# Last FFN of a four-layer trunk: column pairs of its first product by Strassen's seven products, and the second product's weights loaded by use

## The chip, the cores and the metric

One Trainium2 chip, one of its cores. The kernel is launched once. Its time is the device time of that launch in microseconds (us), and lower is better. Engines are named as in the profile: PE is TensorE (matmuls; PEld its weight loads), DVE is VectorE, ACT is ScalarE, POOL is GpSimd, SP is SyncE, whose queue issues most DMAs.

## What is computed

Two layers of an encoder trunk over 512 tokens of 1024 features: a mixer (a short convolution in the first layer, a chunked state-space mixer in the second) and a feed-forward network (FFN) after each, all float32. The change is in the last FFN:

```python
D_MODEL, SEQ, D_FF = 1024, 512, 2816
def swiglu_ffn(h, w_in, w_out):
    gate, up = jnp.split(h @ w_in, 2, axis=-1)
    return (jax.nn.silu(gate) * up) @ w_out
# for each layer, after its mixer:
h = rmsnorm(x, norm_g[i, 2]) * (1.0 + scale) + shift
x = x + gate * rmsnorm(swiglu_ffn(h, f_w_in[i], f_w_out[i]), norm_g[i, 3])
```

`h @ w_in` (512 x 1024 by 1024 x 5632) is called the first product here, the product with `w_out` (512 x 2816 by 2816 x 1024) the second. In the kernel `w1` is `w_in` and `w2` is `w_out` of the last layer.

## The kernel before

**Matmuls in three parts.** A float32 operand is split into a rounded high part (a copy to the type fp32r, on ACT) and the rest (a subtraction on DVE). A product is then three matmuls: high by high, high by low, low by high (`mm3`, L275 to L278). So every weight tile costs an ACT copy and a DVE subtraction of the same size before TensorE can use it.

**First product.** 44 chunks of 128 columns (22 for the gate, 22 for the up half). A chunk (`in_chunk`, L289) is 8 blocks of 128 features times three matmuls of all 512 tokens, accumulated in one PSUM bank. Six chunks (`lead_ps`) are begun in the boundary ahead of the stage with 256 tokens at a time and ended by `rest` (L1678). Two more (`more`) have their weights ready. The other 36 come in 18 pairs: `load_pair` (L1580) loads 256 columns, 1 MB, into a staging tile `wst` (a pool of two), and the splits run two chunks ahead of TensorE. `gate` (L1583) puts SiLU of a gate chunk into a temporary, `up` (L1591) multiplies the up chunk with it into `raw`, and `s13` (L1587) forms sums of `raw` for the second product.

**Second product.** It runs by Strassen's scheme already: `w2` in four blocks b11 to b22, the activations in a11 to a22, 7 products of 11 pairs each, 77 steps of 6 matmuls of 512 columns (`products`, L1639). `w_prep` and `a_prep` split what a pair of steps (a number n from 0 to 38) needs, some steps ahead. The sums of weight blocks are made by DMAs of the POOL queue that add while they write, `add_` (L1656), with the names `t1`, `t2_`, `t3`, `t4`; `behind(n)` (L1743) places them and the output arithmetic by n. `w2` lies in units of one or two pairs (`units`, nine of them): units 0 to 2 in `w2t` tiles, loaded at chunks 8, 14 and 20 of the first product, 3 and 4 in the staging pool near its end, and 5 to 8 in the space of `h` once the first product is over (L1705 to L1710). `t3` needs b12 + b22 in b11's place: ACT's queue loads the one (`t3_load`) and POOL adds the other from memory.

**Order.** In this stage all five engines run in the written order (`manual_schedule`, L1653): on each engine and on each queue an instruction that waits holds up all that stand behind it. A tile that takes the place of an older one waits until the older one's last reader is done.

## Time and profile before

| | |
|---|---|
| three timed runs | 1356.21, 1356.53, 1357.03 us (median 1356.53) |
| profiled execution: span from the first to the last instruction | 1355.3 us, 17419 instructions |
| mean granted TensorE clock | 0.997 |
| HBM read | 192.75 MB |
| plain loads of 1 MB of `w1` | 16 after 1030 us, 5.2 us from issue to landing |
| accumulating DMAs (POOL queue) | 38, 11.54 MB |

The execution was taken by the hardware profiler; only its span is given, and the timed runs lie 1.2 us above it in the median. L12 is line 12 of the kernel. A row of a group gives line, engine, operation, tiles written and read, shape and count, then the busy time and the mean duration in ns, then the idle time just before such instructions and what ended it. A row of the timeline gives start, duration, and in brackets the idle time before it and what ended it; "issue" is a wait for nothing that the profile shows as data. Six columns of a stretch are its length and the busy us of the engines with instruction counts, then the granted clock, the DMA engines' busy share and GB/s.

### The profile page before, as it was taken

To read this page: it belongs to the slowest core of one execution; us is meant where nothing else is said; L and a number is where in the kernel's file an instruction comes from. 1 tells how busy PE (TensorE), PEld (TensorE's weight loads), DVE (VectorE), ACT (ScalarE), POOL (GpSimd) and SP (SyncE) were. 2 spreads that over 40 slices of the span, in tenths; PEclk is the share of its full clock that TensorE was granted. 3 is DMA by queue.
4 is the path that set the end of the run, shared out by engine and by line. 5 is a ranking of instruction groups with operands and counts; after the bars stand their busy time and mean duration, and the time that the engine had idled before them with its cause. 6 is when DMAs were issued, how large, how long until landed. Compare 5 with 4: busy or idle time off the path is not lost.

```text
span 1355.3 us, 17419 instructions
## 1 busy us (share of the span) xinstructions
PE 1339.1 (99%) x6909; PEld 1126.9 (83%) x6909; DVE 898.7 (66%) x1437; ACT 570.1 (42%) x893; POOL 47.0 (3%) x61
## 2 busy tenths in 40 slices
PE   8999999999999999999999999999999999999996
PEld 6788889888888888898888888888899888888885
DVE  5588866777777322658988998897673233336877
ACT  5333355232222211655554455564472212224664
POOL 0000000000000000000000000000000000001231
PEclk9999999999999999999999999999999999999998
DMA  9757760777786323415434334323311455326685
GB/s 311 233 180 231 247 202 4 242 237 245 227 257 201 110 94 94 128 33 162 137 122 128 107 96 132 117 78 121 129 62 63 156 171 172 98 96 196 159 148 120
DMA packets 160565, 204.77 MB, mean 151 GB/s; under 512 B 6868, under 2 KB 112228, under 8 KB 159460
## 3 DMA queue, kind: packets, MB, share of 16 engines
q1 hardware_dynamic: 148512, 176.34, 41.2%
q0 software_dynamic: 6240, 11.54, 5.1%
q10 hardware_dynamic: 5732, 15.79, 3.6%
q8 instruction: 54, 0.88, 0.3%
q14 instruction: 27, 0.22, 0.1%
HBM read 192.75 MB, written 2.24 MB: 144 GB/s over the span
## 4 chain that ended last, share of the span: by engine, by line
PE 93%; issue 2%; SPq 2%; DMA 1%; DVE 1%; ACT 1%; POOL 0%; DVEq 0%; POOLq 0%; ACTq 0%
PE ip L276 19%; PE ip L278 18%; PE ip L277 18%; PE y L378 6%; PE y L379 6%; PE y L380 6%; PE cA L1650 3%; PE li L276 3%; PE li L278 3%; PE li L277 3%; PE li L756 1%; PE yd L1283 1%; PE cD L1650 1%; SPq L611 1%; PE yo L1277 1%
## 5 line engine op out<-in xcount | busy, mean ns | idle before, releaser
L276 PE MATMUL ip<-h,whl 128*128 128x512 f32 x1096 | 431.1, 393 | 0.2 <-DVE cv L863 0.2
L278 PE MATMUL ip<-h,whl 128*128 128x512 f32 x1096 | 427.2, 390 | 0.0
L277 PE MATMUL ip<-h,whl 128*128 128x512 f32 x1096 | 426.8, 389 | 0.0
L222 DVE TENSOR_TENSOR whl<-wst,whl 128x1024 fp32r<-128x1024 f32 x132 | 160.7, 1221 | 133.4 <-ACT whl L221 133.2
L276 PEld LDWEIGHTS ip<-h,whl 128*128 128x128 f32 x1096 | 205.9, 188 | 43.9 <-issue 1.8
L278 PEld LDWEIGHTS ip<-h,whl 128*128 128x128 f32 x1096 | 205.8, 188 | 43.2
L277 PEld LDWEIGHTS ip<-h,whl 128*128 128x128 f32 x1096 | 206.0, 188 | 41.8
L221 ACT CAST whl<-wst 128x1024 fp32r<-128x1024 f32 x132 | 136.6, 1042 | 32.5 <-PE ip L278 23.7
L124 DVE SCALAR_TENSOR_TENSOR ada_acc<-ada_st,csil,ada_acc 128x512 f32<-128x512 f32 x140 | 105.0, 750 | 3.5
L204 DVE TENSOR_TENSOR whlo<-wsto,whlo 128x1024 fp32r<-128x1024 f32 x41 | 49.9, 1224 | 78.5 <-ACT whlo L203 78.4
L276 PE MATMUL li<-h,whl 128*128 128x256 f32 x288 | 83.3, 289 | 0.0
L278 PE MATMUL li<-h,whl 128*128 128x256 f32 x288 | 81.7, 284 | 0.0
L277 PE MATMUL li<-h,whl 128*128 128x256 f32 x288 | 81.6, 283 | 0.0
L203 ACT CAST whlo<-wsto 128x1024 fp32r<-128x1024 f32 x41 | 42.6, 1049 | 76.5 <-PE y L380 71.3
L378 PE MATMUL y<-whlo,ff 128*128 128x512 f32 x176 | 68.7, 390 | 0.0
L380 PE MATMUL y<-whlo,ff 128*128 128x512 f32 x176 | 68.5, 389 | 0.0
L379 PE MATMUL y<-whlo,ff 128*128 128x512 f32 x176 | 68.5, 389 | 0.0
L1142 DVE SCALAR_TENSOR_TENSOR cu<-ip,cols,cu 128x511 f32<-128x511 f32 (+2 forms) x84 | 62.8, 748 | 3.9 <-ACT cu L1139 1.4
L1585 ACT ACTIVATE g<-ip 128x512 f32<-128x512 f32 x18 | 10.8, 598 | 122.1 <-PE ip L278 122.1
L1650 PE MATMUL cA<-whlo,ao 128*128 128x512 f32 x264 | 61.1, 390 | 0.8 <-ACT whlo L1615 0.8
L1650 PEld LDWEIGHTS cA<-whlo,ao 128*128 128x128 f32 x264 | 49.5, 188 | 11.4 <-ACT whlo L1615 1.2
L276 PEld LDWEIGHTS li<-h,whl 128*128 128x128 f32 x288 | 55.3, 192 | 0.0
(281 smaller groups left out, 1928.2 us busy)
## 6 DMA issues: line engine op xcount, KB each, us to landing
ada_st<-in_ada_w_dram SPq DMA_DIRECT2D x96, 512.0 KB, 5.0
wst<-in_f_w_in_dram SPq DMA_DIRECT2D x44, 1024.0 KB, 5.9
wst<-in_m_w_in_dram SPq DMA_DIRECT2D x14, 1024.0 KB, 5.3
wsto<-in_f_w_out_dram SPq DMA_DIRECT2D x10, 1024.0 KB, 5.0
wst<-in_m_w_in_dram SPq DMA_DIRECT2D x20, 512.0 KB, 5.1
wst<-in_a_w_in_dram SPq DMA_DIRECT2D x9, 1024.0 KB, 6.0
csb<-cs_d ACTq DMA_DIRECT2D x8, 1024.0 KB, 5.5
wsto<-in_m_w_out_dram SPq DMA_DIRECT2D x7, 1024.0 KB, 6.5
```

Source lines behind the costliest of these rows:

```text
L124: dve.scalar_tensor_tensor(acc, w, csil[:, k:k + 1], acc, MUL, ADD)
L204: dve.tensor_tensor(dst[:, 1, :nk, :], src, dst[:, 0, :nk, :].bitcast(F32), SUB)
L221: later.append((lambda sw=sw, w=w: act.copy(w[:, 0, :nk, :], sw), lambda sw=sw, w=w: dve.tensor_tensor(w[:, 1, :nk, :], sw, w[:, 0, :nk, : ...
L222: lambda sw=sw, w=w: dve.tensor_tensor(w[:, 1, :nk, :], sw, w[:, 0, :nk, :].bitcast(F32), SUB)))
L276: pe.matmul(dst, w_at(w, 0, kk), a[:, 0, sl], start=start, stop=False)
L277: pe.matmul(dst, w_at(w, 0, kk), a[:, 1, sl], start=False, stop=False)
L278: pe.matmul(dst, w_at(w, 1, kk), a[:, 0, sl], start=False, stop=stop)
L378: pe.matmul(pst, a[:, 0, tk], wt[:, 0, kk, :], start=k == 0, stop=False)
L379: pe.matmul(pst, a[:, 0, tk], wt[:, 1, kk, :], start=False, stop=False)
L380: pe.matmul(pst, a[:, 1, tk], wt[:, 0, kk, :], start=False, stop=k == K - 1)
L1142: dve.scalar_tensor_tensor(u[:, sft:], pst[:, :T - sft], w[3 - sft], u[:, sft:], MUL, ADD)
L1650: pe.matmul(bank[r][sub], a[:, al, q, tk], w[:, hl, q, :], start=first and k == 0, stop=last and k == 2, skip_group_check=True)
```

## The change

The 36 paired chunks become 16 *units* and four plain chunks. A unit is a pair of neighbouring column chunks, gate (even u) or up (odd u). Its four quadrants (feature halves by column chunks) and the four quadrants of `h` (feature halves by token halves, `HALVES`) go through Strassen's seven products P1 to P7, each 4 blocks x 3 matmuls of 256 columns (`product`, `FACTORS`).

- The sums of quadrants of `h` are made once, ahead of the loop: `value` joins high and low part of `h` again, and `t_one` to `t_four` form the four sums and split them into `tq`, which takes the space of `w2t0` and `w2t1`. `va` is a staging tile (`wst`).
- The sums of weight quadrants are made per unit: `fetch(u)` loads five pieces by SP (1.25 MB, rows of 512 bytes) and adds four pieces of 128 KB by `add_` on POOL; `sum_y` and `sum_s` add two more on DVE. `split_x`, `split_y`, `split_z`, `split_s` are the high and low parts of four weight tiles.
- The products of a unit are spread over two turns of the loop (P1, P5, P2, P6, P3 in its own, P7 and P4 in the next). `keep`, `c11`, `c12`, `c22`, `c21` put the four result quadrants together out of three PSUM banks, and end with SiLU or with the product into `raw`.
- All of `w2` is loaded after the units, block by block (`w2_load(i, "b11", ...)`) in the order of use.
- `t3` is a subtraction on POOL (b22 - b11, with b22 already holding the sum) instead of a load and an adding DMA, and stands behind `t4`.

```diff
-        ws, splits, gates = list(more), [(), ()], {}
-        w2t = [fb.tile([P, 2, 2, D], F32, tag=f"w2t{i}", name=f"w2t{i}") for i in range(2)]
-        w2t += [fb.tile([P, 1, 2, D], F32, tag="w2t2", name="w2t2")]
+        gates = {}
+        tq = [fb.tile([P, 2, 2, 4, 256], F32R, tag=f"w2t{i}", name=f"tq{i}") for i in range(2)]
+        sums_w = fb.tile([P, 2, 2, 4, P], F32, tag="w2t2", name="sg")
         raw = fb.tile([P, NF, T], F32, tag="raw", name="raw")
...
+        def w2_load(i, *names):
             u = units[i]
-            t = w2t[i] if i < 3 else wst_p.tile([P, 1, 2, D], F32, tag="wst", name="w2s")
-            for q in range(len(u)):
-                dma(t[:, q, :, :], w2_rows(u[q])[:, 0])
-            rows_of[i] = (t[:, :, 0, :], t[:, :, 1, :])
+            for name in names:
+                r, c = int(name[1]) - 1, int(name[2]) - 1
+                dma(b_(i, name), w2_rows(u[0], len(u))[:, :, r, c * T:(c + 1) * T])
...
+        UN = 16
+        LO, HI = HALVES
+        FACTORS = {"P1": ("X", 0, "A"), "P2": ("X", 4, "B"), "P3": ("S", 0, "C"), "P4": ("Z", 4, "A"),
+                   "P5": ("Y", 0, "C"), "P6": ("Y", 4, "A"), "P7": ("Z", 0, "A")}
+        staged, wts, banks, outs = {}, {}, {}, {}
+        def w1_cols(u, f, kh=None):
+            c0 = u % 2 * DFF + (4 + u // 2 * 2 + f) * P
+            rows = slice(0, D) if kh is None else slice(kh * T, (kh + 1) * T)
+            return w1[rows, c0:c0 + P].rearrange("(k p) f -> p k f", p=P)
+        def add_(dst, src):
+            pool.dma_start(dst, src, accum_op=ADD)
+        def fetch(u):
+            st, sg = wst_p.tile([P, 16, P], F32, tag="wst", name="wsu"), sums_w[:, u % 2]
+            staged[u] = st, sg
+            dma(st[:, 0:8, :], w1_cols(u, 0))
+            if u < UN:
+                dma(sg[:, 0], w1_cols(u, 1, 0))
+            if u:
+                dma(st[:, 8:12, :], w1_cols(u - 1, 0, 0))
+            for b in (0, 2):
+                if u < UN:
+                    add_(sg[:, 0, b:b + 2, :], w1_cols(u, 1, 1)[:, b:b + 2, :])
+                if u:
+                    add_(st[:, 8 + b:10 + b, :], w1_cols(u - 1, 1, 0)[:, b:b + 2, :])
+            if u:
+                dma(st[:, 12:16, :], w1_cols(u - 1, 1, 1))
...
+        def split_x(u):
+            wts["X", u] = whole()
+            split(wts["X", u], staged[u][0][:, 0:8, :])
+        def split_y(u):
+            wts["Y", u] = whole()
+            split(wts["Y", u], staged[u][1].rearrange("p s k f -> p (s k) f"))
+        def split_z(u):
+            wts["Z", u] = whole()
+            split(wts["Z", u], staged[u + 1][0][:, 8:16, :])
+        def split_s(u):
+            wts["S", u] = fo.tile([P, 2, 4, P], F32R, tag="ao", name="wss")
+            split(wts["S", u], staged[u][0][:, 4:8, :])
+        def sum_y(u):
+            st, sg = staged[u]
+            dve.tensor_add(sg[:, 1], sg[:, 0], st[:, 0:4, :])
+        def sum_s(u):
+            st, sg = staged[u]
+            dve.tensor_add(st[:, 4:8, :], sg[:, 1], st[:, 4:8, :])
...
+        def product(u, q):
+            kind, k0, r = FACTORS[q]
+            if q in ("P1", "P5", "P2"):
+                banks[r, u] = (aux_ps if r == "B" else mm_ps)(f"s{r}")
+            dst, w = banks[r, u][:, LO], wts[kind, u]
+            for k in range(4):
+                for i, (wl, al) in enumerate(((0, 0), (0, 1), (1, 0))):
+                    pe.matmul(dst, w[:, wl, k0 + k, :], moving(q, k, al), skip_group_check=True,
+                              start=q in ("P1", "P5", "P2") and k == 0 and i == 0, stop=k == 3 and i == 2)
...
+        def c11(u):
+            dve.tensor_add(out_of(u, 0)[:, LO], banks["B", u][:, LO], out_of(u, 0)[:, LO])
+        def c12(u):
+            o, f = out_of(u, 0), 4 + u // 2 * 2
+            dve.tensor_add(o[:, HI], banks["C", u][:, LO], o[:, HI])
+            if u % 2:
+                dve.tensor_mul(o, o, gates[f])
+            else:
+                gates[f] = o
+                act.activation(o, o, AF.Silu)
...
-            def t3_load(i):
-                for q, p in enumerate(units[i]):
-                    dma_s(b_(i, "b11", q), w2_rows(p)[:, 0, 0, T:])
             def t3(i):
-                for q, p in enumerate(units[i]):
-                    add_(b_(i, "b11", q), w2_rows(p)[:, 0, 1, T:])
+                pool.tensor_tensor(b_(i, "b11"), b_(i, "b22"), b_(i, "b11"), SUB)
...
+            va = wst_p.tile([P, 4, T], F32, tag="wst", name="va")
+            vb = [fo.tile([P, 2, T], F32, tag="ao", name="vb") for _ in range(2)]
+            fetch(0)
+            def value(j):
+                dst = va[:, j, :] if j < 4 else vb[j // 2 - 2][:, j % 2, :]
+                dve.tensor_add(dst, h[j][:, 0, :].bitcast(F32), h[j][:, 1, :].bitcast(F32))
...
+            def t_one():
+                dve.tensor_tensor(va[:, :, LO], va[:, :, LO], va[:, :, HI], SUB)
+                t_low(tq_of(0, slice(0, 4)), va[:, :, LO])
+            def t_two(b):
+                k = slice(2 * b, 2 * b + 2)
+                dve.tensor_tensor(va[:, k, HI], vb[b][:, :, HI], va[:, k, HI], SUB)
+                dve.tensor_add(vb[b][:, :, HI], vb[b][:, :, HI], va[:, k, LO])
+                t_low(tq_of(1, k), vb[b][:, :, HI], -1.0)
+            def t_three():
+                t_low(tq_of(2, slice(0, 4)), va[:, :, HI])
+            def t_four(b):
+                k = slice(2 * b, 2 * b + 2)
+                dve.tensor_tensor(vb[b][:, :, LO], vb[b][:, :, HI], vb[b][:, :, LO], SUB)
+                t_low(tq_of(3, k), vb[b][:, :, LO])
...
             for i, f in ((0, 0), (2, 0), (1, 1), (3, 1), (4, 2), (5, 3)):
                 rest(i)
-                (up if i in (2, 3) else gate)(f, lead_ps[i])
-            tiles = []
-            K = 2 * NF - 6
-            for k in range(K):
-                if k % 2 == 0 and k < K - 4:
-                    load_pair(k // 2 + 1)
-                if k in (8, 14, 20):
-                    w2_load((8, 14, 20).index(k))
-                if k in (K - 4, K - 2):
-                    w2_load(3 + (k - K + 4) // 2)
-                if k in (K - 12, K - 10, K - 8):
-                    t1((k - K + 12) // 2)
-                tiles.append(in_chunk(ws[k], h))
-                q, j = divmod(k - 3, 4)
-                if j < 2 and k > 2:
-                    gate(4 + 2 * q + j, tiles[k - 1])
-                elif k:
-                    up(2 + 2 * q + j, tiles[k - 1])
-                if k < K - 2:
-                    for op in splits[k + 2]:
+                if i in (2, 3):
+                    up(f, lead_ps[i])
+                else:
+                    gate(f, lead_ps[i])
+                if i == 1:
+                    for j in range(4):
+                        value(j)
+                elif i == 3:
+                    t_one()
+                elif i == 4:
+                    for j in range(4, 8):
+                        value(j)
+            acc = in_chunk(more[0], h)
+            split_x(0)
+            for b in range(2):
+                t_two(b)
+            sum_y(0)
+            split_y(0)
+            t_three()
+            fetch(1)
+            acc2 = in_chunk(more[1], h)
+            sum_s(0)
+            up(2, acc)
+            split_s(0)
+            for u in range(UN):
+                v = u - 1
+                last = u == UN - 1
+                if u + 2 <= UN:
+                    fetch(u + 2)
+                elif last:
+                    tail = []
+                    n12 = load_w([(w1, 21 * P, P), (w1, DFF + 20 * P, P)], later=tail)
+                product(u, "P1")
+                if u:
+                    c12(v)
+                else:
+                    up(3, acc2)
+                    for b in range(2):
+                        t_four(b)
+                split_x(u + 1)
+                if u:
+                    product(v, "P7")
+                keep(u, "A", 0, LO)
+                if not last:
+                    sum_y(u + 1)
+                product(u, "P5")
+                if u:
+                    c22(v)
+                product(u, "P2")
+                keep(u, "C", 1, HI)
+                if not last:
+                    sum_s(u + 1)
+                if u:
+                    product(v, "P4")
+                c11(u)
+                split_z(u)
+                product(u, "P6")
+                if u:
+                    c21(v)
+                if last:
+                    for op in tail[0]:
                         op()
+                    n3 = load_w([(w1, DFF + 21 * P, P)], later=tail)
                 else:
-                    a_prep(k - K + 2)
-                    w_prep(k - K + 2)
-            up(NF - 1, tiles[-1])
+                    split_y(u + 1)
+                product(u, "P3")
+                keep(u, "A", 0, HI)
+                if not last:
+                    split_s(u + 1)
+            u = UN - 1
+            w2_tile(0)
+            w2_load(0, "b11", "b21")
+            w2_tile(2)
+            w2_load(2, "b11", "b21", "b22", "b12")
+            w2_load(0, "b22", "b12")
+            tiles = [in_chunk(wts["X", UN], h)]
+            c12(u)
+            for op in tail[1]:
+                op()
+            product(u, "P7")
+            gate(20, tiles[0])
+            tiles.append(in_chunk(n12[0], h))
+            c22(u)
+            for op in tail[2]:
+                op()
+            product(u, "P4")
+            gate(21, tiles[1])
+            w2_tile(1)
+            w2_load(1, "b11")
+            w2_tile(3)
+            w2_load(3, "b11")
+            tiles.append(in_chunk(n12[1], h))
+            c21(u)
+            a_prep(0)
+            w_prep(0)
+            tiles.append(in_chunk(n3[0], h))
+            up(20, tiles[2])
+            w2_tile(4)
+            w2_load(4, "b11")
+            w2_load(1, "b21")
+            a_prep(1)
+            w_prep(1)
+            up(21, tiles[3])
...
+            late = range(5, len(units))
+            for i in late:
+                w2_load(i, "b11")
+            w2_load(3, "b21")
+            w2_load(4, "b21")
+            for i in late:
+                w2_load(i, "b21")
+            for i in (1, 3, 4, *late):
+                w2_load(i, "b22", "b12")
             for n in (2, 3):
                 w_prep(n)
             a_prep(2)
-            for i in range(3, len(units)):
+            for i in (0, 2, 1, *range(3, len(units))):
                 t1(i)
...
-                    if n == 8 + i:
-                        t3_load(i)
-                    if n == 17:
-                        t3(i)
-                if n == 18:
+                if n == 17:
                     for i in range(len(units)):
                         t4(i)
+                    for i in range(len(units)):
+                        t3(i)
                 for t in range(2):
                     if n == 5:
                         got["11", t] = t2("c11")
```

More of the change, by code (lines that the diff above doesn't have):

```diff
@@ L1578, in a_ @@
             return v[:, :, c, slice(0, 256) if name[1] == "1" else slice(256, T)]
-        def load_pair(p):
-            ws.extend(load_w([(w1, p % 2 * DFF + (4 + p // 2 * 2) * P, 256)], later=splits))
         def gate(f, pst):
@@ new lines, in split, with whole @@
+        def split(dst, src):
+            act.copy(dst[:, 0], src)
+            dve.tensor_tensor(dst[:, 1], src, dst[:, 0].bitcast(F32), SUB)
+        def whole():
+            return whl_p.tile([P, 2, 8, P], F32R, tag="whl", name="whl")
+        def split_x(u):
[7 more added lines that the diff above has]
+            split(wts["Z", u], staged[u + 1][0][:, 8:16, :])
@@ new lines, in out_of, with keep @@
+        def out_of(u, f):
+            if (u, f) not in outs:
+                outs[u, f] = raw[:, 4 + u // 2 * 2 + f, :] if u % 2 else t2("g")
+            return outs[u, f]
+        def keep(u, r, f, part):
+            act.copy(out_of(u, f)[:, part], banks[r, u][:, LO])
+        def c11(u):
[8 more added lines that the diff above has]
+                act.activation(o, o, AF.Silu)
@@ new lines, in c22, with c21 @@
+        def c22(u):
+            o = out_of(u, 1)
+            dve.scalar_tensor_tensor(o[:, HI], banks["A", u][:, LO], -1.0, o[:, HI], MUL, SUB)
+            if u % 2 == 0:
+                act.activation(o[:, HI], o[:, HI], AF.Silu)
+        def c21(u):
+            o, f = out_of(u, 1), 5 + u // 2 * 2
+            act.activation(o[:, LO], banks["A", u][:, LO], AF.Copy if u % 2 else AF.Silu, scale=-1.0)
+            if u % 2:
+                dve.tensor_mul(o, o, gates[f])
+                raw_done(f)
+            else:
+                gates[f] = o
@@ new lines, in tq_of @@
+            def tq_of(i, ks):
+                return [tq[i // 2][:, i % 2, hl, ks, :] for hl in range(2)]
+            def t_one():
[6 more added lines that the diff above has]
+                t_low(tq_of(1, k), vb[b][:, :, HI], -1.0)
```

34 lines of the change are left out of this document (25 added, 9 removed).

## The prediction

> **What bounds the kernel now.** I read the page's busy shares and the chain that ended last, then busy time by stage, then the instructions of each engine in order of time.
>
> ```profile
> PE 1339.1 (99%) x6909; PEld 1126.9 (83%) x6909; DVE 898.7 (66%) x1437; ACT 570.1 (42%) x893; POOL 47.0 (3%) x61
> PE 93%; issue 2%; SPq 2%; DMA 1%; DVE 1%; ACT 1%; POOL 0%; DVEq 0%; POOLq 0%; ACTq 0%
> ```
>
> TensorE is busy 99% of the span and carries 93% of the chain. By stage of the last FFN (first product, second product; the columns are us, PE, PEld, DVE, ACT and POOL busy, clock, DMA share, GB/s):
>
> ```profile
> 1032.20:1238.20 206.00, 206.00 (x910) 170.63 (x909) 68.75 (x73) 50.23 (x61) 5.20 (x5) 1.00 0.41 130
> 1238.20:1345.20 107.00, 105.83 (x465) 86.70 (x463) 84.67 (x135) 68.56 (x123) 30.23 (x33) 1.00 0.75 159
> ```
>
> In the first product TensorE has no gap, while VectorE works a third of the time, GpSimd 2.5% and the DMA engines 41%. So any time taken out of TensorE there is gained, as long as the others keep up. What a matmul costs is the distance between starts, not its duration, because they overlap:
>
> ```profile
> 1235.71 0.39 PE L278 MATMUL ip<-h,whl 128*128 128x512 f32 x1
> ...
> 1238.43 0.39 PE L278 MATMUL ip<-h,whl 128*128 128x512 f32 x1
> 1238.66 1.52 PE L1650 MATMUL cA<-whlo,ao 128*128 128x512 f32 x6
> ```
>
> Twelve 512-column matmuls between the two L278 rows: 2.72/12 = 0.2267 us each. The second product starts at 1238.66. The boundary before this stage has 256-column matmuls, sixty of them between these two rows:
>
> ```profile
> 1018.12 0.28 PE L278 MATMUL li<-h,whl 128*128 128x256 f32 x1
> ...
> 1025.32 0.28 PE L278 MATMUL li<-h,whl 128*128 128x256 f32 x1
> ```
>
> 7.20/60 = 0.120 us each. A half-width matmul costs 53% of a full one.
>
> **The change: TensorE.** A pair of column chunks is now 2 x 24 = 48 matmuls of 512 columns, 48 x 0.2267 = 10.88 us. As one Strassen unit it is 7 products x 12 = 84 matmuls of 256 columns, 84 x 0.120 = 10.08 us. An eighth of the arithmetic goes, but the half-width price gives back part: 0.80 us a unit, 12.8 us for 16 units. That is all there is to win.
>
> **The change: DVE and ACT.** Rows of the operations it uses (mean ns after the busy time):
>
> ```profile
> L222 DVE TENSOR_TENSOR whl<-wst,whl 128x1024 fp32r<-128x1024 f32 x36 | 44.0, 1221 | 73.3 <-ACT whl L221 73.3
> L1588 DVE TENSOR_TENSOR s1t<-raw 128x512 f32<-128x512 f32 x5 | 3.5, 692 | 0.2
> L1588 DVE TENSOR_TENSOR s1t<-raw 128x256 f32<-128x256 f32 x1 | 0.4, 426 | 0.0
> L1740 DVE SCALAR_TENSOR_TENSOR x<-c,ss,x 128x512 f32<-128x512 f32 x4 | 3.0, 752 | 0.1
> L221 ACT CAST whl<-wst 128x1024 fp32r<-128x1024 f32 x36 | 36.8, 1047 | 28.1 <-PE ip L278 23.7 <-DMA wst<-in_f_w_in_dram 4.5
> L1615 ACT CAST whlo<-w2h 128x512 fp32r<-128x512 f32 x28 | 16.6, 620 | 13.3 <-PE cA L1650 5.3 <-DMA w2h<-w2h 2.7 <-PE cC L1650 2.1
> L1585 ACT ACTIVATE g<-ip 128x512 f32<-128x512 f32 x18 | 10.8, 598 | 122.1 <-PE ip L278 122.1
> ```
>
> VectorE per unit: three splits of 1024 (3.66), one split and two weight sums of 512 (2.08), three combinations of 256 (1.28), and on average one product of 512 and half a row of the s13 sums (1.0): 8.0 us. ScalarE: 3 x 1.05 + 0.62, four 256-column copies at about 0.40 and half a SiLU: 5.9 us. Both fit under 10.08 us, VectorE without much room; beside TensorE they cost nothing as long as what they read has arrived.
>
> **The change: GpSimd's accumulating DMAs.** The weight sums that Strassen needs are made by `add_` in `fetch`: four a unit on the POOL queue, each 2 x 128 rows of 512 bytes (128 KB); a unit's plain loads are 1.25 MB. The kernel already has accumulating DMAs, and their rows show how many can be under way. POOL in order of time, first the 256-row adds (w2t), then what follows:
>
> ```profile
> 1246.30 2.66 POOL L1657 DMA_DIRECT2D w2h<-w2h  x3 [14.57 <-DMA w2h<-in_f_w_out_dram]
> 1251.71 0.86 POOL L1657 DMA_DIRECT2D w2h<-w2h  x1 [2.75 <-issue]
> ...
> 1272.34 2.16 POOL L1657 DMA_DIRECT2D w2t<-w2t  x2 [7.71 <-DVE ao L1629]
> 1277.71 1.78 POOL L1657 DMA_DIRECT2D w2s<-w2s  x2 [3.22 <-issue]
> ...
> 1288.88 0.89 POOL L1657 DMA_DIRECT2D w2t<-in_f_w_out_dram  x1 [1.58 <-issue]
> ...
> 1312.10 1.22 POOL L1657 DMA_DIRECT2D w2t<-w2t  x1 [2.58 <-issue]
> 1317.47 2.14 POOL L1657 DMA_DIRECT2D w2t<-w2t  x2 [4.14 <-issue]
> ```
>
> Three adds of 128 rows go out together and the fourth waits 2.75 us for "issue", no data dependence. A 256-row add and a 128-row add go out together and the next waits 3.22. After a 256-row add at 1312.10 a second 256-row add waits 4.14 us, and starts 5.37 us after the first. So room for adds in flight ends between 384 and 512 rows: **adds of 256 rows run one at a time**. Every `add_` of the change has 256 rows, all follow each other on POOL, and so a unit lasts at least four full round trips of an add.
>
> What a round trip of 512-byte rows costs, no row shows. DMA rows of two stretches, the adds of 2 KB (1311 to 1333 us) and plain loads of 512-byte rows alone (549 to 559.5 us):
>
> ```profile
> q0 software_dynamic: 1664, 3.09, 82.5%
> ```
>
> ```profile
> q1 hardware_dynamic: 5200, 2.62, 94.0%
> wst<-in_m_w_in_dram SPq DMA_DIRECT2D x4, 512.0 KB, 5.4
> ```
>
> A 2 KB packet of an add takes 0.825 x 16 x 22 us / 1664 = 174 ns of an engine; a plain 512-byte packet 0.94 x 16 x 10.5 / 5200 = 30 ns. Of the 5.37 us, 16 packets on each of 16 engines are 2.78, and 2.59 is fixed (issue, start, receipt). With 512-byte rows the moving part is at least 16 x 30 ns = 0.49 (round trip 3.08) and at most 2.78 (5.37). I take 60 ns, a plain packet read twice, for source and destination: 0.96, so 3.55; and 0.3 for the loads, whose 2560 packets a unit (2560 x 30/16 = 4.8 us) share the engines: **3.85 us an add, 15.4 us a unit**, against TensorE's 10.08.
>
> [...]
>
> Could VectorE or buffers bind first? `fetch(u+2)` reuses the staging tile that `split_s(u)` frees, about 6 us of splits after unit u's last add, and the loads land some 5 us later: 11 us, less than the 15.4 that POOL then spends on unit u+1. POOL's queue stays full.
>
> **The change: the start.**
>
> ```profile
> 1019.65 0.37 SPq L212 DMA_DIRECT2D wst<-in_f_w_in_dram  x1
> ```
>
> ```profile
> 1032.19 1.29 DVE L1592 TENSOR_TENSOR raw<-li,g 128x512 f32<-128x512 f32 x2 [12.57 <-PE li L278]
> ```
>
> The first `up` waits until the boundary's last matmul although its input is older, and in VectorE's order the eight `value` adds now stand behind it. So VectorE's new chain starts at 1032.2: two `up` 1.3, eight values 5.2, `t_one` 1.22 + 1.05 (waiting for ACT) + 1.22, `split_x` 1.22, `t_two` twice 2.75, `sum_y` 0.69, `split_y` 2.27, `t_three` 1.22: 20.9 us, with a few hand-overs about 1053.7. TensorE reaches unit 0 at 1032.1 + 2 x 5.44 = 1043.0, while behind `t_three` stand four 512-column steps of 0.69, `t_four` twice 2.0 and `split_x` 1.22 before unit 1 can begin: 1061.7 instead of 1050.2, a start late by 11.5 us. `fetch(1)` waits for `t_three`, since its tile is the one `va` used; its loads land 5 us later and the first of its adds starts at about 1058.5. From there sixty adds to the end of unit 15's: 60 x 3.85 = 231, at 1289.5; then `split_z`, `c21` and the last unit's matmuls, 12 us, and the tail (four chunks of 5.44, two products of 1.44) 24.6.
>
> Second product starts at 1058.5 + 231 + 12 + 24.6 = 1326.1 instead of 1238.7: **+87.4 us**.
>
> **The change: the second product.** Loads of w2 come after the units, 4.5 MB beside the tail and 6.5 MB beside the second product; its 105.8 us of matmuls hide them: at 250 to 340 GB/s the last land some 22 to 26 us in, and b22 is first split 21 us in. Cost 0; 5 if that fails. The eleven loads and eleven adds of `t3` go; nine subtractions on GpSimd come, behind the nine t4 adds.
>
> ```profile
> 890.20 1.29 POOL L1299 TENSOR_TENSOR accg<-accg,sqg 128x512 f32<-128x512 f32 x1 [39.05 <-ACT sqg L1297]
> ```
>
> t4 begins where t3 did (1288.88, 50 us in) and takes the 18 us that it takes now (1312.1 to 1330.2); the first three subtractions 2.6 + 2.6 + 1.3; the split 1.3: 76 us in. Its matmuls are due 75 us in. I put +1; bounds 0 and +8.
>
> **Sum.** The span is 1355.3 and the median of the runs 1356.53; the 1.2 us around the span stay. 1356.5 + 87.4 + 1 = 1445.
>
> **The rivals.**
> (a) *The adds are hidden* because several are in flight or each takes under 2.52 us (a quarter of 10.08). For it: POOL is 3% busy, and the adds here are a quarter of 512 KB. Against it: the 4.14 us wait and the 2.59 fixed. Then TensorE's 10.08 sets the unit, but the late start stays: 1061.7 + 15 x 10.08 + 24.6 = 1237.5, 1.2 us earlier, and +1 in the second product: 1356; with VectorE's 8 us in strict order at 10.5 a unit, 1363. [...]
> (b) *Faster*: as (a), and the start is covered too, so TensorE goes through: 1043.0 + 161.3 + 21.8 = 1226.1, 12.6 us earlier: 1344. It decides only if an add is under 2.52 us and VectorE has the terms by 1043. Against it both rows above.
> (c) *The adds are dearer*: a 512-byte packet of an add costs what a 2 KB one does, 174 ns: 5.37 us an add, 21.5 a unit, 1058.5 + 322.2 + 36.6 = 1417.3: 1536.
>
> **Chances.** The forecast (an add of 3.08 to 4.9 us, 1399 to 1508) 0.77; (a) 0.13, of it 0.03 below by over 0.2%, 0.03 within and 0.07 above; (b) 0.03; (c) 0.07. 0.2%, 2.7 us, is about what a measurement of this kernel can tell from no change. Faster 0.06, same 0.03, slower 0.91. The range runs from below the cheapest add of the forecast to an add of 4.9 us: 1390 to 1508.
>
> **What would show it.** Right: TensorE idle about 5 us in each unit, waits of `split_z` or `sum_y` on accumulating DMAs, POOL's adds starting 3 to 4.5 us apart with "issue" ahead of each, matmuls still 0.120 apart inside a product. Wrong: adds of 256 rows starting 2 us apart or less; VectorE busy all the time; TensorE without gaps after unit 1; or a second product far from 107 us.

## The result and the profile after

| | before | after |
|---|---|---|
| median (runs) | 1356.78 us (4: 1356.21 to 1357.86) | 1492.16 us (4: 1491.37 to 1494.87) |
| span of the profiled execution | 1355.3 us | 1489.5 us |
| first product from 1032.1, second product | 206.6 and 107 us | 326 and 121.4 us |

The changed kernel takes 1.1 times as long, 95% interval 1.0985 to 1.1016: slower by 135 us, where +88.5 was forecast.

Busy shares and the chain that ended last, from the page after:

```profile
PE 1365.2 (92%) x7485; PEld 1177.1 (79%) x7485; DVE 984.8 (66%) x1570; ACT 617.1 (41%) x995; POOL 128.7 (9%) x123
PE 73%; issue 11%; DVE 4%; DMA 4%; POOL 3%; ACT 2%; SPq 2%; POOLq 0%; ACTq 0%; DVEq 0%
```

TensorE falls from 99% to 92% of a longer span, and "issue" rises from 2% to 11% of the chain: 164 us in which an engine waited for nothing that the profile shows as data. Busy time by stage shows where: first the units (from unit 1 to the last add), then a stretch in the second product (columns as before):

```profile
1074.00:1333.00 259.00, 179.91 (x1245) 177.07 (x1246) 111.46 (x155) 80.96 (x140) 70.60 (x58) 0.83 0.51 104
```

```profile
1428.00:1444.00 16.00, 5.31 (x17) 3.54 (x16) 9.24 (x5) 4.17 (x7) 13.38 (x10) 0.67 0.21 42
```

Over the units no engine is full: TensorE works 69%, VectorE 43%, the DMA engines 51%. So something else sets their pace, and POOL's queue is the place to look. In the second stretch GpSimd is the busy one, with 13.4 of 16 us.

**The units.** POOL in order of time, all accumulating DMAs of `fetch`:

```profile
1057.48 1.21 POOL L1619 DMA_DIRECT2D sg<-in_f_w_in_dram  x1 [55.11 <-DMA wsu<-in_f_w_in_dram]
...
1201.08 1.21 POOL L1619 DMA_DIRECT2D wsu<-in_f_w_in_dram  x1 [2.52 <-DVE whl L1640]
1206.62 1.23 POOL L1619 DMA_DIRECT2D sg<-in_f_w_in_dram  x1 [4.33 <-issue]
1210.48 1.21 POOL L1619 DMA_DIRECT2D wsu<-in_f_w_in_dram  x1 [2.63 <-issue]
1214.31 1.22 POOL L1619 DMA_DIRECT2D sg<-in_f_w_in_dram  x1 [2.61 <-issue]
...
1320.46 1.22 POOL L1619 DMA_DIRECT2D wsu<-in_f_w_in_dram  x1 [2.74 <-issue]
```

The adds go out singly. From the first row to the last it is 60 adds: (1320.46 - 1057.48) / 60 = 4.383 us each, 17.5 us a unit. They are not alike: 3.83 to 3.86 us apart in the middle rows, 5.54 for the add at 1201.08, which runs beside the unit's plain loads (SP issues them from 1201.3 on). TensorE in the same unit:

```profile
1200.27 1.60 PE L1684 MATMUL sA<-h,whl 128*128 128x256 f32 x12
1201.71 1.60 PE L1684 MATMUL sA<-tq,whl 128*128 128x256 f32 x12
...
1204.59 1.60 PE L1684 MATMUL sB<-h,whl 128*128 128x256 f32 x12
1211.32 4.78 PE L1684 MATMUL sA<-tq,whl 128*128 128x256 f32 x24 [5.13 <-DVE raw L1710]
1215.94 1.60 PE L1684 MATMUL sC<-h,wss 128*128 128x256 f32 x12
```

A product of twelve takes 1.44 us, 0.120 a matmul as forecast. Then TensorE is idle for 5.13 us; over the 259 us it is 79.1, about 5.3 a unit. That equals the forecast by chance: the unit takes 17.5 us where 15.4 was forecast, and TensorE is busy for 12.2 of them where 10.08 was, because the matmuls right behind each stop are slower (0.19 us each in the row of 1211.32; last section). The releaser, L1710, is `c22`, a short VectorE operation that frees the bank; it is not the cause. What VectorE did before it is in the list of waits from 1015 us on (engine, tile and line, releaser: total, times, longest):

```profile
DVE sg L1663 <- issue: 50.1, 7, 7.6
...
DVE sg L1663 <- DMA sg<-in_f_w_in_dram: 44.3, 8, 9.2
```

L1663 is `sum_y` and stands ahead of `c22` in VectorE's order. Fifteen times, 94 us in all, it waits, with `c22` behind it and TensorE behind that. Eight of these waits end by the accumulated tile. The other seven are put down to "issue"; read beside POOL's rows they look like the same wait: the one that ends at 1210.24 does so 3.6 us after the add of 1206.62 went out.

**The second product.** Matmuls into bank cA, first to last start:

```profile
L1775 PE MATMUL cA<-whlo,ao x264: 387/389/468, 1358.1 to 1479.2; 128*128 128x512 f32 x132
```

It starts at 1358.1 and takes 121.4 us instead of 107. The three engines at the place where that happens, POOL, VectorE and TensorE:

```profile
1427.30 0.86 POOL L1619 DMA_DIRECT2D w2h<-w2h  x1 [1.03 <-issue]
1427.86 6.21 POOL L1785 TENSOR_TENSOR w2t<-w2t 128x1024 f32<-128x1024 f32 x3
1433.74 2.78 POOL L1785 TENSOR_TENSOR w2s<-w2s 128x512 f32<-128x512 f32 x2
1436.20 5.18 POOL L1785 TENSOR_TENSOR w2h<-w2h,w2h 128x512 f32<-128x512 f32 x4
```

```profile
1425.94 0.69 DVE L1741 TENSOR_TENSOR whlo<-w2h,whlo 128x512 fp32r<-128x512 f32 x1 [0.82 <-ACT whlo L1740]
1434.76 7.18 DVE L1741 TENSOR_TENSOR whlo<-w2t,whlo 128x512 fp32r<-128x512 f32 x1 [8.13 <-ACT whlo L1740]
1441.86 0.68 DVE L1754 TENSOR_TENSOR ao<-s1t,ao 128x512 fp32r<-128x512 f32 x1
```

```profile
1435.30 1.22 PE L1775 MATMUL cD<-whlo,ao 128*128 128x512 f32 x2 [4.62 <-ACT ao L1753]
1442.59 5.37 PE L1775 MATMUL cD<-whlo,ao 128*128 128x512 f32 x13 [6.07 <-DVE ao L1754]
```

The first `t3` subtractions are ready at 1434.07 (1427.86 + 6.21). ACT's copy and split wait for them, and TensorE is idle for 4.62 us. Then one split of 128x512 takes 7.18 us on VectorE; the same operation takes 0.69 nine us earlier. It ends at 1441.9, half a microsecond after GpSimd's last subtraction (1436.20 + 5.18 = 1441.4), and TensorE is idle for another 6.07 us.

Both parts together: first product 326 - 206.6 = +119.4, second +14.4, sum 133.8; the spans differ by 134.2.

### The profile page after: what moved, and what is told of

It is laid out like the page before. It is cut to its first block, busy times and chain, and to the rows that moved or that the text cites. A ratio compares the mean times of both kernels' runs of the same rounds, so it can differ in the third digit from the quotient of the medians.

```text
span 1489.5 us, 19188 instructions
## 1 busy us (share of the span) xinstructions
PE 1365.2 (92%) x7485; PEld 1177.1 (79%) x7485; DVE 984.8 (66%) x1570; ACT 617.1 (41%) x995; POOL 128.7 (9%) x123
## 4 chain that ended last, share of the span: by engine, by line
PE 73%; issue 11%; DVE 4%; DMA 4%; POOL 3%; ACT 2%; SPq 2%; POOLq 0%; ACTq 0%; DVEq 0%
PE ip L276 13%; PE ip L278 13%; PE ip L277 13%; PE y L378 6%; PE y L380 6%; PE y L379 6%; PE li L276 2%; PE li L278 2%; PE li L277 2%; PE sA L1684 2%; DMA wsu<-in_f_w_in_dram 2%; PE cA L1775 2%; PE li L756 1%; POOL wsu L1619 1%; PE yd L1283 1%
## 5 line engine op out<-in xcount | busy, mean ns | idle before, releaser
L276 PE MATMUL ip<-h,whl 128*128 128x512 f32 x840 | 331.3, 394 | 0.2 <-DVE cv L863 0.2
L278 PE MATMUL ip<-h,whl 128*128 128x512 f32 x840 | 327.3, 390 | 0.0
L277 PE MATMUL ip<-h,whl 128*128 128x512 f32 x840 | 327.1, 389 | 0.0
L1684 PE MATMUL sA<-tq,whl 128*128 128x256 f32 x576 | 102.6, 349 | 91.1 <-DVE raw L1710 38.9
L276 PEld LDWEIGHTS ip<-h,whl 128*128 128x128 f32 x840 | 157.8, 188 | 33.8 <-issue 1.8
L278 PEld LDWEIGHTS ip<-h,whl 128*128 128x128 f32 x840 | 157.7, 188 | 33.4
L277 PEld LDWEIGHTS ip<-h,whl 128*128 128x128 f32 x840 | 157.8, 188 | 31.6
L1684 PEld LDWEIGHTS sA<-tq,whl 128*128 128x128 f32 x576 | 97.5, 258 | 94.5 <-DVE raw L1710 40.3
L222 DVE TENSOR_TENSOR whl<-wst,whl 128x1024 fp32r<-128x1024 f32 x99 | 120.3, 1220 | 59.9 <-ACT whl L221 59.7
L221 ACT CAST whl<-wst 128x1024 fp32r<-128x1024 f32 x99 | 103.0, 1041 | 3.2 <-DMA wst<-in_m_w_in_dram 2.0
L1640 DVE TENSOR_TENSOR whl<-wsu,whl 128x1024 fp32r<-128x1024 f32 x33 | 40.4, 1223 | 62.4 <-ACT whl L1639 62.4
L1639 ACT CAST whl<-wsu 128x1024 fp32r<-128x1024 f32 x33 | 34.5, 1044 | 97.8 <-PE sA L1684 45.6
L1663 DVE TENSOR_TENSOR sg<-sg,wsu 128x512 f32<-128x512 f32 x16 | 11.1, 692 | 94.5 <-issue 50.1
L378 PE MATMUL y<-whlo,ff 128*128 128x512 f32 x176 | 68.7, 390 | 0.0
L380 PE MATMUL y<-whlo,ff 128*128 128x512 f32 x176 | 68.5, 389 | 0.0
```

Of the source, the lines that this page charges most:

```text
L221: later.append((lambda sw=sw, w=w: act.copy(w[:, 0, :nk, :], sw), lambda sw=sw, w=w: dve.tensor_tensor(w[:, 1, :nk, :], sw, w[:, 0, :nk, : ...
L222: lambda sw=sw, w=w: dve.tensor_tensor(w[:, 1, :nk, :], sw, w[:, 0, :nk, :].bitcast(F32), SUB)))
L276: pe.matmul(dst, w_at(w, 0, kk), a[:, 0, sl], start=start, stop=False)
L277: pe.matmul(dst, w_at(w, 0, kk), a[:, 1, sl], start=False, stop=False)
L278: pe.matmul(dst, w_at(w, 1, kk), a[:, 0, sl], start=False, stop=stop)
L378: pe.matmul(pst, a[:, 0, tk], wt[:, 0, kk, :], start=k == 0, stop=False)
```

## The experiments

The theory behind the prediction (A): room for adds in flight makes the adds of 256 rows go one at a time. Its rivals: the bytes or the DMA engines set their pace, or VectorE's order does. For the second product: `t3` on GpSimd is the cause (D), by coming late or by stopping VectorE, against the late loads of `w2`. Every ratio below is to the kernel before (medians of 1356.4 to 1356.6 us).

**Twice the room.** The kernel's constant for it, and with it two small tiles (`gr`, shown, and `ones`) put elsewhere:

```diff
-        gr = tmp.tile([KD, P], F32, tag="gr", name="gr", bufs=1)
+        gr = t2("gr")[:KD, :P]
...
-    nc = _bacc.Bacc("TRN2", target_bir_lowering=False, num_devices=1, dynamic_dma_scratch_size=1024)
+    nc = _bacc.Bacc("TRN2", target_bir_lowering=False, num_devices=1, dynamic_dma_scratch_size=2048)
```

> [...] Theory A (room lets one 256-row add run at a time, four round trips of 4.4 us set the unit's 17.5 us): three adds fit now, POOL's adds start 1.3 to 2.2 us apart when their data is there, and a unit falls to what TensorE and VectorE need in order, 10.1 to 12 us; that is 5.5 to 7.4 us less in each of 15 units: 1380 to 1410 us. Rival B (the DMA engines with their 512-byte rows, or VectorE's strict order, set the unit and the waits of POOL are only a symptom): adds come no closer on average than 3.5 us and the time stays above 1460.

Measured 1394.46 us, ratio 1.028 (1.025 to 1.031): 98 us of the 135 are gone. POOL, and the matmuls of the second product:

```profile
1156.09 1.22 POOL L1620 DMA_DIRECT2D sg<-in_f_w_in_dram  x1 [4.26 <-DMA sg<-in_f_w_in_dram]
1157.60 1.21 POOL L1620 DMA_DIRECT2D wsu<-in_f_w_in_dram  x1 [0.29 <-DMA wsu<-in_f_w_in_dram]
1158.81 1.24 POOL L1620 DMA_DIRECT2D sg<-in_f_w_in_dram  x1
1159.78 1.50 POOL L1620 DMA_DIRECT2D wsu<-in_f_w_in_dram  x1
```

```profile
L1776 PE MATMUL cA<-whlo,ao x264: 388/389/796, 1264.3 to 1382.7; 128*128 128x512 f32 x132
```

The same four adds with the same bytes now start 1.0 to 1.5 us apart, and the second product starts 93.8 us earlier. "issue" ahead of the units' adds falls from 157 us in all to 6. A is right: room, not bytes, set the pace of 17.5 us (B falls as its cause). What is left is a wait before the first add of a unit, here for the plain load whose tile it adds to, in other units for a VectorE operation. A unit still takes 11.3 us and not 10.08 (fifteen units between the first `sg` adds at 1057.52 and the last unit's at 1226.34); the third step below takes up the difference.

**Half the size.** Eight adds of 128 rows instead of four of 256, in the old room:

```diff
-            for b in (0, 2):
+            for b in range(4):
                 if u < UN:
-                    add_(sg[:, 0, b:b + 2, :], w1_cols(u, 1, 1)[:, b:b + 2, :])
+                    add_(sg[:, 0, b:b + 1, :], w1_cols(u, 1, 1)[:, b:b + 1, :])
                 if u:
-                    add_(st[:, 8 + b:10 + b, :], w1_cols(u - 1, 1, 0)[:, b:b + 2, :])
+                    add_(st[:, 8 + b:9 + b, :], w1_cols(u - 1, 1, 0)[:, b:b + 1, :])
```

> The changed kernel with eight adds of 128 rows a unit in place of four of 256, in the room of before. Theory A (room counted in rows, 384 fit): three small adds are in flight, one starts every 1.1 to 1.6 us, eight take 9 to 13 us, the unit falls from 17.5 to 11 to 13.5: 1390 to 1430 us. Rival C (one add at a time whatever its size): eight round trips of 3.3 us or more make 26 us a unit: above 1600.

Measured 1418.94 us, ratio 1.046 (1.043 to 1.0491), the second product from 1285.7 on. POOL:

```profile
1135.75 0.86 POOL L1619 DMA_DIRECT2D wsu<-in_f_w_in_dram  x1 [1.13 <-issue]
1136.29 1.23 POOL L1619 DMA_DIRECT2D sg<-in_f_w_in_dram  x1
1136.84 1.57 POOL L1619 DMA_DIRECT2D wsu<-in_f_w_in_dram  x1
1140.98 0.86 POOL L1619 DMA_DIRECT2D sg<-in_f_w_in_dram  x1 [2.57 <-issue]
```

Twice as many DMAs for the same bytes, and 73 us faster: three go out together before "issue" returns. It isn't the number of adds that counts (C falls). Nor is it their bytes: in the kernel before, adds of 256 rows of 2 KB went singly too, and three of 128 such rows together. It is the rows in flight: 384 went together there, 512 didn't.

**No adds.** The block of adds is removed:

```diff
-            for b in (0, 2):
-                if u < UN:
-                    add_(sg[:, 0, b:b + 2, :], w1_cols(u, 1, 1)[:, b:b + 2, :])
-                if u:
-                    add_(st[:, 8 + b:10 + b, :], w1_cols(u - 1, 1, 0)[:, b:b + 2, :])
```

> Leaves out the four accumulating DMAs of every unit (the weight sums lack their second summand); all else stays. Theory A: without POOL the unit is TensorE's 10.08 us or a little more where VectorE's order holds it up, at most 12: 1370 to 1405 us, of which 14 are the second product. Rival B (loads or VectorE set the unit): above 1440, with TensorE still idle some 5 us in each unit.

Measured 1376.61 us, ratio 1.0148 (1.0118 to 1.0178). Busy time over the units:

```profile
1074.00:1219.00 145.00, 144.13 (x1196) 143.48 (x1195) 103.96 (x147) 76.99 (x129) 0.00 (x0) 1.00 0.46 126
```

TensorE is full, so VectorE's and ScalarE's work does fit beside it (104 and 77 of 145 us), and without adds nothing breaks the units. Still the kernel is slower than before: its second product starts at 1243.4, not earlier than 1238.7, and has the stop by `t3`. The gain of 12.8 us is spent at the start.

**`t3` on VectorE.**

```diff
-                pool.tensor_tensor(b_(i, "b11"), b_(i, "b22"), b_(i, "b11"), SUB)
+                dve.tensor_tensor(b_(i, "b11"), b_(i, "b22"), b_(i, "b11"), SUB)
```

> The changed kernel with t3's nine subtractions on VectorE instead of GpSimd, at the same place in the order. The second product took 121.4 us instead of 107. Theory D (VectorE's split at 1434.8 lasts 7.18 us instead of 0.69 while GpSimd subtracts, and waits for GpSimd's queue before it): the second product goes back to 107 to 111 us: 1478 to 1483. Rival E (the later loads of w2 cost the 14 us): stays at 1490 to 1494.

Measured 1482.12 us, ratio 1.0926 (1.0894 to 1.0958), 10 us less than after: the second product runs from 1358.6 to about 1471, 112 us. All `w2` loads stand where they stood, so `t3` on GpSimd is a cause (D) and the loads don't make these 10 us (E falls). Some 5 us are left. Spreading `t3` takes only about 2 of them: with `t3` spread and the old room (the last run below) the second product takes 110 us, with `t3` spread and the doubled room 106.

**More loads beside the adds.** In 14 units, 0.5 MB more, into a part of `raw` that isn't in use yet:

```diff
             dma(st[:, 0:8, :], w1_cols(u, 0))
+            if 1 < u < UN:
+                dma(raw[:, 20:22, :].rearrange("p a (k f) -> p (a k) f", f=P), w1_cols(u, 0))
```

> The changed kernel with one more plain load of 512 KB in 512-byte rows in each of units 2 to 15, into rows of raw that nothing has used yet; the results are not touched. In the profile after, three of a unit's four adds start 3.8 us apart and the one that runs beside the unit's loads 5.4 to 6.3. Theory A (an add shares the DMA engines with the loads beside it, and as adds are strictly one after the other the unit pays for it): 0.5 MB is about 2 us of the engines, so 1 to 2 us a unit, 14 units: 1506 to 1522 us. Rival F (the long add is long for another reason, for instance it waits for its own load to land): 1489 to 1495.

Measured 1509.79 us, ratio 1.1129 (1.1107 to 1.1151). POOL:

```profile
1209.42 1.21 POOL L1619 DMA_DIRECT2D wsu<-in_f_w_in_dram  x1 [2.68 <-DVE whl L1642]
1216.24 1.23 POOL L1619 DMA_DIRECT2D sg<-in_f_w_in_dram  x1 [5.61 <-issue]
1220.11 1.21 POOL L1619 DMA_DIRECT2D wsu<-in_f_w_in_dram  x1 [2.64 <-issue]
```

The add beside the loads takes 6.82 us here, more than any in the changed kernel (at most 6.36), and the next stays at 3.87. Over all 62 adds the spacings of 4.3 us and more go from 18 to 25, with a mean of 5.63 and 5.74, while the others stay at 3.85 and 3.89: the added load mostly makes a further add dear, and not the same one dearer. The unit's own loads beside them make these adds dear (F falls).

**Towards a better kernel.** Three steps on top of the doubled room, each with the ones before it. First, `t3` on VectorE, a few at a time instead of all at n = 17:

```diff
-                    for i in range(len(units)):
-                        t3(i)
+                for i in ((2, 0), (1, 3), (4, 5), (6, 7), (8,))[n - 18] if 18 <= n <= 22 else ():
+                    t3(i)
```

> Twice the room for adds (as e1, 1394.5 us) and t3's subtractions on VectorE, two per step n from 18 to 22 instead of all at once. Theory D (GpSimd's subtractions cost the second product 11 to 14 us): 1380 to 1385 us, second product 107 to 109 us. Rival E (late loads of w2): above 1390.

Measured 1385.15 us, ratio 1.021 (1.019 to 1.0231), at the upper edge of what was expected; the second product takes 106 us (1266.0 to 1372) instead of 118.7. The late loads of `w2` stand where they stood, so they cost nothing (E falls).

Second, the start: the eight `value` adds, `t_one`, `split_x`, `sum_y` and `split_y` go between the `rest` steps, and the first two `up` behind them, out of VectorE's way (`split_s` also goes ahead of the third `up`):

```diff
             for i, f in ((0, 0), (2, 0), (1, 1), (3, 1), (4, 2), (5, 3)):
                 rest(i)
-                if i in (2, 3):
-                    up(f, lead_ps[i])
-                else:
+                if i not in (2, 3):
                     gate(f, lead_ps[i])
-                if i == 1:
+                if i in (0, 1):
                     for j in range(4):
-                        value(j)
-                elif i == 3:
+                        value(4 * i + j)
+                elif i == 2:
                     t_one()
...
+            up(0, lead_ps[2])
+            up(1, lead_ps[3])
             acc = in_chunk(more[0], h)
```

> As e6, and the terms of h and the weights of unit 0 are made ahead of the first two up instead of behind them, in the 12 us in which VectorE idles until the boundary's last matmul; fetch(1) goes out as soon as va is free. The late start (TensorE idle 12.7 us before unit 1 in e1) should fall to 0 to 4 us: 1369 to 1375 us. If the start were hidden by later waits anyway: 1380 or more.

Measured 1372.42 us, ratio 1.0116 (1.0096 to 1.0137), as expected; the second product starts at 1256.2, 9.8 us earlier.

Third, the order inside a unit: loads and adds in the order in which they are used (first `sg`, which `sum_y` needs), and `sum_y` and `sum_s` behind `c11` instead of ahead of the operations that free banks:

```diff
-            dma(st[:, 0:8, :], w1_cols(u, 0))
             if u < UN:
                 dma(sg[:, 0], w1_cols(u, 1, 0))
             if u:
                 dma(st[:, 8:12, :], w1_cols(u - 1, 0, 0))
+            dma(st[:, 0:8, :], w1_cols(u, 0))
             for b in (0, 2):
                 if u < UN:
                     add_(sg[:, 0, b:b + 2, :], w1_cols(u, 1, 1)[:, b:b + 2, :])
+            for b in (0, 2):
...
                 c11(u)
+                if not last:
+                    sum_y(u + 1)
+                    sum_s(u + 1)
```

> As e7, and in each unit the loads and adds of sg go first and sum_y and sum_s stand behind c11, so that VectorE's order does not wait for an add that is needed only at the end of the turn. With a unit at 10.1 to 10.6 us instead of about 11.4 in e1: 1353 to 1363 us; where TensorE's 10.08 is reached in all units 1349. If the loads' landing, not the order, sets the 11.4: 1366 or more.

Measured 1350.67 us (4 runs, 1350.34 to 1351.5), ratio 0.9957 (0.994 to 0.9973): below the 1353 to 1363 and near the 1349 of the text, and faster than both kernels, than the one before by 5.8 us. Busy time over the units, and the second product:

```profile
1062.00:1208.00 146.00, 144.47 (x1199) 143.82 (x1198) 105.74 (x147) 76.70 (x130) 65.25 (x54) 1.00 0.84 174
```

```profile
L1777 PE MATMUL cA<-whlo,ao x264: 387/389/467, 1233.0 to 1338.9; 128*128 128x512 f32 x132
```

TensorE is full, with all adds done; the second product starts 5.7 us earlier than before the change and takes the same time. Of the 12.8 us that the sixteen units can win, 5.7 arrive; where the rest goes wasn't followed. The three edits of the order were made together, so their shares aren't known. POOL, a unit's four adds:

```profile
1109.57 2.45 POOL L1620 DMA_DIRECT2D sg<-in_f_w_in_dram  x2 [2.64 <-DVE raw L1712]
1111.19 2.07 POOL L1620 DMA_DIRECT2D wsu<-in_f_w_in_dram  x1
1114.36 1.20 POOL L1620 DMA_DIRECT2D wsu<-in_f_w_in_dram  x1 [1.10 <-issue]
```

Three go out in a row, and the fourth waits 1.10 us for "issue": double the room holds three adds of 256 rows, as the old room held three of 128.

**Late or stopped?** In the changed kernel, `t3` ahead of `t4` instead of behind it, 20 us earlier:

```diff
                 if n == 17:
                     for i in range(len(units)):
+                        t3(i)
+                    for i in range(len(units)):
                         t4(i)
-                    for i in range(len(units)):
-                        t3(i)
```

> The changed kernel with the nine subtractions of t3 on GpSimd ahead of the nine t4 adds instead of behind them. Two readings of the 14 us in the second product: G (they only come too late behind 20 us of t4 adds): ahead of them they are done 14 us after n = 17, in time for n = 27, and the second product goes back to 107 to 110 us: 1478 to 1482. H (while GpSimd subtracts without a break, VectorE's splits stand still, as the 7.18 us row suggests): the same stall comes earlier, VectorE loses most of the 14 us at n = 17 to 21 and TensorE, with three to four steps of 2.7 us prepared, 3 to 10 of them: 1483 to 1491.

Measured 1493.05 us, ratio 1.1007 (1.0975 to 1.1039). This missed: it lies outside both ranges, above them. POOL, VectorE and TensorE:

```profile
1408.06 6.27 POOL L1785 TENSOR_TENSOR w2t<-w2t 128x1024 f32<-128x1024 f32 x3
...
1416.42 5.19 POOL L1785 TENSOR_TENSOR w2h<-w2h,w2h 128x512 f32<-128x512 f32 x4
```

```profile
1407.14 15.03 DVE L1741 TENSOR_TENSOR whlo<-w2s,whlo 128x512 fp32r<-128x512 f32 x2
1422.09 0.68 DVE L1754 TENSOR_TENSOR ao<-raw,ao 128x512 fp32r<-128x512 f32 x1
```

```profile
1422.83 7.35 PE L1775 MATMUL cA<-whlo,ao 128*128 128x512 f32 x19 [10.90 <-DVE ao L1754]
```

Two splits of 0.69 take 15.03 us, and end 0.6 us after GpSimd's last subtraction (1421.6). In this stretch no engine waits for a subtraction's result; VectorE stands still for the whole row of subtractions, and TensorE is idle for 10.90 us, about the 10.7 of the changed kernel (H had put 3 to 10). The second product takes as long as there. In the run with twice the room, too, TensorE was idle for 10.96 us while the subtractions ran, though they ended 67 us into the second product. So lateness alone falls, and the stop is the mechanism.

**The order without the room.** The kernel of the third step with the old room (and the two small tiles where they were):

```diff
-    nc = _bacc.Bacc("TRN2", target_bir_lowering=False, num_devices=1, dynamic_dma_scratch_size=2048)
+    nc = _bacc.Bacc("TRN2", target_bir_lowering=False, num_devices=1, dynamic_dma_scratch_size=1024)
```

> As e8 (1350.7 us) with the room of before (1024 bytes): the early terms, the order and t3 on VectorE stay. Theory A (the serial adds set the unit whatever the order): sixty adds at 4.2 to 4.4 us again, the chain beginning about 13 us earlier than in the changed kernel, t3 worth 10 to 14: 1465 to 1475 us. If the order had done it: below 1400.

Measured 1459.41 us, ratio 1.0759 (1.0728 to 1.0791), 6 us under what was expected. POOL:

```profile
1257.62 1.22 POOL L1619 DMA_DIRECT2D wsu<-in_f_w_in_dram  x1 [5.08 <-DVE g L1698]
1261.29 1.21 POOL L1619 DMA_DIRECT2D wsu<-in_f_w_in_dram  x1 [2.44 <-issue]
1265.04 1.22 POOL L1619 DMA_DIRECT2D sg<-in_f_w_in_dram  x1 [2.54 <-issue]
```

Singly again, 3.7 us apart here and 4.40 in the mean of all, against 4.38 in the changed kernel. The expectation counted sixty adds in the chain; two adds of unit 1 go out ahead of it, at 1005 and 1009 us, and two adds fewer are 8.8 us. Without the room the other steps together bring 33 us; the room brings another 109 and decides.

## Why the prediction was right or wrong, step by step

**TensorE's price: right for a TensorE that doesn't stop.** 12 matmuls of 256 columns in 1.44 us, 10.08 us a unit. Without adds, TensorE was full at that price. Behind a stop the price was higher (0.19 and 0.23 us a matmul), which the prediction left out; see the start.

**DVE and ACT fit: right.** The working's terms for ScalarE add up to 5.7 us and not 5.9; per unit of 10.1 us, the run without adds has 7.2 us of VectorE (forecast 8.0) and 5.4 of ScalarE. The run without adds and the one with the new order have TensorE at 99% of the units.

**Adds of 256 rows run one at a time: right**, for the reason given. The three-and-wait pattern of 128-row adds in the trace of before was enough to see it; doubled room and halved adds confirm it from both sides.

**The length of an add: right in kind, too short.** 3.85 us was forecast, 4.383 measured, and 60 x 0.533 = 32 us of the 46.4 that the forecast lacks (1491.4 of the profiled run, less 1445) are this term. Both its parts were too small. Of the 61 spacings between the 62 adds, 43 are under 4.3 us, with a mean of 3.85; this is the add that no load delays, where I took 3.55, so with 2.59 fixed the moving part of 512-byte rows is 1.26 us by this estimate, where I took 0.96. For the loads I put 0.3 an add in the mean; it is 4.383 - 3.85 = 0.53, all of it on the 18 long spacings. That the add alone costs just what was forecast for the whole is chance. The bounds, 3.08 and 5.37, held it.

**The start: right for the adds, too short for TensorE.** The first add after `t_three` was put at 1058.5 and came at 1057.48. With the measured add the forecast's own sum gives 1058.5 + 60 x 4.383 + 12 + 24.6 = 1358.1, and the second product began at 1358.1. To the last us this is luck: the chain began 1.0 us earlier than put, and what follows the sixtieth add took 37.6 us instead of 36.6. TensorE reached unit 1 at 1065.56 and not at 1061.7. Its idle times in unit 0 were right (5.65, 0.47 and 5.20 us, together 11.3 against 11.5), but the matmuls between them were slower than the 0.120 us that was put throughout: the ten from 1051.18 were 0.23 apart, the twelve from 1060.80 0.227. The chain of adds hides this. In the run without adds it shows: unit 1 begins at 1065.88, and the second product at 1243.4, where rival (a)'s sum has 1237.5. That the late start alone takes the gain, as (a) had it, holds; it takes more than the gain.

**The second product: wrong.** "I put +1; bounds 0 and +8"; it was +14.4. The working was right within 2 us as far as it went: `t4` ended 70 us in (forecast 68), and the first subtractions were ready 76 us in (forecast 74.5). Two things were missed. The matmuls were due earlier than I put them: TensorE ran dry at 1430.7, 72.6 us in, and stood for 4.62 us. And I costed GpSimd's subtractions only as work of GpSimd: they stopped VectorE, which held the next split for 6.5 us more and TensorE for 6.07. Together 10.7; about 2.3 of the other 3.7 are the slow matmuls after the second stop (last section). A second product far from 107 us was one of the prediction's own signs of being wrong, and this one came true. The runs show the stop: a split took 7.18 us instead of 0.69 beside the subtractions, and two took 15.03 in the run with `t3` ahead. VectorE was held not for one instruction of GpSimd but until the last of the row had ended, 0.56 us before the split did in both; the row has nine of them.

**The sum.** 32 for the add and 13.4 for the second product are 45.4 of the 46.4; 1 us is not followed. No rival came true.

## What to carry to other kernels

Before work is moved to accumulating DMAs, count how many rows fit in flight: "issue" ahead of nearly every DMA of the POOL queue, while no engine is full, was the sign here that they go singly, and then each costs its whole round trip (3.85 us for 128 KB). Work put on an idle GpSimd isn't always free when VectorE runs beside it (7.18 us for a split of 0.69 here); look at VectorE's durations in that stretch, not only at GpSimd's. And when a restructured stage saves an eighth of the arithmetic, price the start, the order and the half-width instructions first: here they took all of it, and careful placing brought back 5.8 of 12.8 us.

## What the runs showed of the hardware

- **Room for accumulating DMAs.** With the constant at 1024 adds of 256 rows went one at a time, 4.383 us each in the mean, and three of 128 rows went together (1135.75 to 1136.84 us in the run with halved adds) before a wait of 2.57 us; at 2048 three of 256 rows went together and the fourth waited 1.10 us. What the doubled room costs elsewhere was not measured.
- **VectorE's splits stood still while GpSimd subtracted.** One split took 7.18 us instead of 0.69, two took 15.03. Splits and subtractions both read two tiles; whether other VectorE operations stop too, no run here shows. ScalarE didn't: its casts of 128x512 beside the same subtractions took 0.61 and 0.62 us, against 0.62 without them.
- **Matmuls behind the stops were slower at first.** After 5.13 us without work, 24 matmuls of 256 columns took 1215.94 - 1211.32 = 4.62 us, 0.19 apart instead of 0.120, at a granted clock of 0.59 (1211.3 to 1215.9); after 6.07 us, 13 of 512 columns were 0.40 apart instead of 0.2267, at 0.56 (1442.6 to 1447.8). In unit 0 of the changed kernel, after 5.20 us:

```profile
1060.80 2.93 PE L1684 MATMUL sA<-tq,whl 128*128 128x256 f32 x12 [5.20 <-ACT g L1694]
1063.52 2.20 PE L1684 MATMUL sC<-h,wss 128*128 128x256 f32 x12
1065.56 1.59 PE L1684 MATMUL sA<-h,whl 128*128 128x256 f32 x12
```

The first twelve are 2.72/12 = 0.227 us apart, 1.9 times the 0.120, at a granted clock of 0.50 (1060.8 to 1063.5); the second twelve 0.17, at 0.67 (1063.5 to 1065.6); from 1065.6 to 1066.9 the clock is 1.00 again. In the units the adds hide it; at the start it costs the run without adds about 4 us (an estimate: unit 1 begins there 23.0 us after unit 0, of which 11.2 are idle, 60 x 0.120 = 7.2 are matmuls at full pace and 3 x 0.16 what the last one ahead of an idle time lasts beyond 0.120), and in the second product the 13 matmuls add 13 x (0.40 - 0.2267) = 2.3 us to the stop.
